# One queue for the turned pieces, pairs of groups four steps apart, and three smaller moves in a two-layer decoder trunk

## The chip, the core and the metric

The kernel runs on one core of one Trainium2 chip. The metric is the device time of one execution in microseconds, as the median of several runs. A profile comes from one execution of its own, taken with the hardware profiler.

The core's engines each run their instructions in order: TensorE (PE) multiplies matrices, VectorE (DVE) and ScalarE (ACT) work elementwise, GpSimd (POOL) and SyncE (SP) here only issue transfers. Transfers are also issued from ScalarE's queue. Each of these three has one queue of its own, and all of them move data over the same 16 DMA engines.

## The reference

Two layers over x of 256 tokens by 2048 features, all in float32:

```
layer 0:  h = rms_norm(x);  x += concat(mixer A(h), mixer B(h)) @ w_out     # gated spatial mixing, HGRN2 recurrence
          h = rms_norm(x);  x += (silu(conv3(h @ w_up)_a) * conv3(h @ w_up)_b) @ w_down
layer 1:  h = rms_norm(x);  x += (attention(h) * sigmoid(gate)) @ w_out     # 16 heads, QK-norm, forgetting bias
          h = rms_norm(x);  x += the same gated FFN with its own weights
```

Mixer A normalises its values v per head by their root mean square (a sum of squares over 128 columns) and mixes them along the tokens. In the attention, a logit per head and token gives log f; its cumulative sum c over the tokens enters the scores as c[t] - c[s]. The FFN has a hidden width of 5632, and conv3 is a causal convolution of width three along the tokens.

## The kernel before, in words

**Steps.** Every product of activations and weights is made from streamed weights. A weight tile w of 128x1024 (512 KB) is loaded on SP's queue (`weights`, L182, the load at L195), rounded by ScalarE into wh (L206), and VectorE makes the rest wl = w - wh (L211). The activations stand as such pairs too, and TensorE makes three products for each pair (L287 to L289 in `project_four`, L267 to L269 in `project_tok`), twelve matmuls of 512 columns for a tile. Such a tile is called a step here. In the mixers w has four buffers, and wh and wl three each; in the FFN every second tile uses a further pool with two of each (L182 to L190). The stationary operand is the activation, so the result has tokens in its partitions. A group of four output tiles (512 features) takes 8 steps over k = 0 to 15, and stands in two PSUM banks, one for each half of the tokens.

**Turning.** Where the next operation needs features in the partitions, the group is turned (`transposed`, L305): VectorE transposes blocks of 32x32 into a tile tmp (L308), and sixteen small transfers of 32 KB move the blocks across the partitions (L314). They go alternately to SP's queue and to GpSimd's, eight each. The last turned tile of the whole program uses three queues instead. In both FFNs tmp has one buffer, so the next tile can be transposed only when all sixteen pieces of the one before have landed. The turned tile is called turn in the mixers and zt in the FFN.

**Order.** A list of generators interleaves the work: `tick` (L121) runs once for each step and moves every pending generator on by one yield. After a tile is turned, its readers are put LAG = 6 steps later (LAST = 7 for the last group of a stage): the convolution in the FFN (L155 by way of `copy_in`, then L989 and L990), the scaled copies of queries and keys (also L155), the gates of the recurrence (L101), and the residual sum (L158) with the next norm's splits (L322, L326, L333, L336). A scheduler in the framework orders each engine's instructions within what the program's order and hand-written order edges leave free.

**Pairs.** The first two groups of an output projection and of an FFN's up-projection are interleaved (`project_pair`, L292), because they start before the last four k tiles of the activations are there: k 0 to 11 of the first (six steps), k 0 to 11 of the second, then k 12 to 15 of the first (two steps) and of the second. The first group so ends two steps before the second. The attention mixer starts in the same manner (L774): k 0 to 11 of the first queries, then of the first keys together with the gate columns (`keys_gate`, L754; its 528 columns take narrower matmuls, L770 and L771), then k 12 to 15 of both. In `keys_gate` the sixteen gate columns come on GpSimd's queue (L761), the rest on SP's (L762).

**Gate rows.** `forget` (L787) makes the cumulative sums, writes them to DRAM (L806) and loads them back into all 128 partitions, all sixteen heads in one transfer of 2 MB (L807). `attend` subtracts them from the scores.

**Values.** In mixer A the sums of squares of the values, their root and the scaling (L486 to L495) stand in the program directly, ahead of `mixes` (L510), which waits three ticks and then mixes a head per tick (L498).

**Start and end.** ScalarE's queue issues the first x tile, the norm's columns pp and the second x tile (L84 to L86), while SP's queue starts with the first weights. At the end, `add_y` (L1024) turns the FFN's last four groups, adds them to x (L158) and `finish_x` (L1048) sends x out; four of the output tiles are instead made feature by feature (L214, L1074 to L1077), so that they need no turning.

Of the kernel before, what the change touches and what calls it, by code (L numbers as in the profile page):

```python
# [8 lines left out]
F32 = mybir.dt.float32  # L9
# [3 lines left out]
ALU = mybir.AluOpType  # L13
AX = mybir.AxisListType

P = 128
S = 256
D = 2048
KT = D // P
NH = 8  # L20
# [6 lines left out]
LAST = 7  # L27
WAIT = 2
JOIN = 12
EPS = 1e-6  # L30
WARM = 7
AHEAD = {2: 2, 4: 4, 6: 6}
# [21 lines left out]
def tile_trunk(ctx: ExitStack, tc: tile.TileContext, x, pp_d, cst_d, mlev_d, msk_d,  # L54
               w_v, w_f, w_g, w_i, w_q, w_u, w_abo, w_cf, w_cqkv, w_cg, w_co, w_up, w_dn, spw_d, spb_d, out):
    nc = tc.nc
    V, SC, PE = nc.vector, nc.scalar, nc.tensor
# [10 lines left out]
    def nm(base):  # L68
        count[0] += 1
        return f"{base}_{count[0]}"  # L70
# [10 lines left out]
    ones = cp.tile([P, P], F32, tag="ones", name="ones")  # L81
    one1 = cp.tile([P, LANE], F32, tag="one1", name="one1")[:, 0:1]

    SC.dma_start(*fetch[0])  # L84
    SC.dma_start(pp[:, 0:C_FFN], pp_d[:, 0:C_FFN])
    SC.dma_start(*fetch[1])  # L86
    V.memset(ones, 1.0)
# [54 lines left out]
    def after(n, g):  # L142
        soon.append([n, g])
# [27 lines left out]
        while flight or queue or free or soon:  # L171
            tick()

    deep = {"pool": None, "turn": 0}

    def in_order(r, key="dma"):
        if key in deep:
# [113 lines left out]

    def project_pair(wa, wb, acts, shift=0):  # L292
        pa, pb = banks_for(), banks_for()
        for part in ((0, JOIN), (JOIN, KT)):
            for w4, ps in ((wa, pa), (wb, pb)):
                project_four(w4, acts, KT, shift=shift, ps=ps, part=part)
                if part[1] == KT:
                    yield ps

    def output(w, acts, shift=0):  # L300
        yield from project_pair(w[0:4], w[4:8], acts, shift)
# [3 lines left out]
    def transposed(src, tmp, dst, queues=None):  # L305

        for T in range(2):
            V.transpose(tmp.rearrange("p (b m i t) -> p b m i t", b=4, m=4, t=2)[:, :, :, :, T],  # L308
                        src(T).rearrange("p (m b j) -> p b m j", m=4, b=4))
        n = 2 * BLK  # L310
        for a in range(4):
            for b in range(4):
                qs = queues or (nc.sync, nc.gpsimd)
                qs[(a + b) % len(qs)].dma_start(dst[BLK * b:BLK * (b + 1), :, a * n:(a + 1) * n],  # L314
                                  tmp[BLK * a:BLK * (a + 1), b * 4 * n:(b + 1) * 4 * n]
                                  .rearrange("p (m r) -> p m r", m=4))
# [103 lines left out]
    def mixer_ab(norm):  # L420
# [61 lines left out]
                        .to_broadcast([P, NH, P]), ALU.mult)  # L482

        ss = hp.tile([P, LANE], F32, tag="ss", name="ss")
        for g in range(2):
            for T in range(2):  # L486
                i = (2 * g + T) * 4
                j = hp.tile([P, 512], F32, tag="smk", name=nm("junk"), bufs=1)
                sumsq(ss[:, i:i + 4], gv[g][:, T], j)
        rsq(ss[:, 0:2 * NH], ss[:, 0:2 * NH], P)  # L490
        for g in range(2):
            for T in range(2):
                i = (2 * g + T) * 4
                v4 = gv[g][:, T].rearrange("p (h d) -> p h d", d=P)
                V.tensor_tensor(v4, v4, ss[:, i:i + 4].unsqueeze(2).to_broadcast([P, 4, P]), ALU.mult)  # L495
        mg = [keep("mg") for _ in range(NH)]

        def mix(h):  # L498
# [9 lines left out]
                                   ALU.mult, ALU.add)  # L508

        def mixes():  # L510
            yield
            yield
            yield
            for h in range(NH):
                mix(h)
                yield
# [230 lines left out]
    def mixer_c(norm):  # L747
# [23 lines left out]
                        deep["main"] = PE.matmul(pb[T][:, 0:S], a_, t[:, CH + S:n], start=begin, stop=end)  # L771

        first = banks_for()
        for part in ((0, JOIN), (JOIN, KT)):  # L774
            project_tok(w_cqkv[0], norm, ps=first, part=part)
            keys_gate(part)
        drain()
        depth[0] = 2
        Rt = norm.Rt
# [3 lines left out]

        ct = hp.tile([P, 2, 2 * CH], F32, tag="ct", name="ct")[..., 0:CH]
        cb = hp.tile([P, CH * S], F32, tag="big", name="cb").rearrange("p (h s) -> p h s", s=S)

        def forget():  # L787
            f, fa, fc, on = (hp.tile([P, S], F32, tag=t, name=t)[0:CH] for t in ("f", "fa", "fc", "on"))
            ft = hp.tile([P, 2, LANE], F32, tag="ft", name="ft")
            V.memset(on, 1.0)  # L790
            for T in range(2):
                SC.activation(ft[:, T, 0:CH], pa[T][:, 0:CH], AF.Copy, scale=Rt[:, T:T + 1])
            yield
            ps = bank()
# [12 lines left out]
            nc.gpsimd.dma_start(cb, cd.partition_broadcast(P))  # L807
            yield
            ps = bank()
            for T in range(2):  # L810
                turn_in(ps[:, T * CH:(T + 1) * CH], fc[:, T * P:(T + 1) * P], ident[0:CH, 0:CH])
            V.tensor_copy(ct, ps[:, 0:2 * CH].rearrange("p (t c) -> p t c", t=2))
# [382 lines left out]
```

## Time and profile before

| | |
|---|---|
| time, median of 3 runs | 2315.13 us (2314.61 to 2317.67) |
| the profiled execution's own time | 2317.44 us |
| its span | 2315.7 us |
| TensorE busy (modelled ends) | 2292.7 us, 99% |
| VectorE, ScalarE, GpSimd busy | 67%, 57%, 15% |
| granted TensorE clock, mean | 0.996 |
| moved by DMA | 481 MB, 208 GB/s |
| pieces of turned tiles (L314) | 638 on SP, 637 on GpSimd, 5 on ScalarE |

The span is the part of the execution that the trace covers. In a timeline row stand the start in us from the span's start, the time in us, the engine, the line, the operation, output and input, the count of merged instructions, and in brackets how long the engine was idle before, with what ended it. SPq and ACTq are the queues' own issues. PEld is the weight load of TensorE, which overlaps the matmuls. Matmul times overlap too, since they are pipelined: the distance between two starts is what one costs.

### The profile page before, as it was taken

How to read it: one execution, taken by the hardware profiler on the slowest of the kernel's cores; microseconds unless marked ns; L12 is line 12 of the kernel's file. 1: busy time of each engine (PE TensorE's matmuls, PEld its weight loads, DVE VectorE, ACT ScalarE, POOL GpSimd, SP SyncE). 2: the span in 40 equal slices, each digit the busy share in tenths (PEclk: the TensorE clock that was granted, in tenths of full speed). 3: DMA queues.
4: the chain of work that ended last, by engine and by line, in shares of the span. 5: the costliest groups of instructions: out<-in, count | busy, mean ns of one | idle time of the engine just before them, and what ended most of it. 6: DMA issues, size and time to landing. Idle time of an engine off the chain costs nothing.

```text
span 2315.7 us, 31427 instructions
## 1 busy us (share of the span) xinstructions
PE 2292.7 (99%) x10370; PEld 1903.9 (82%) x10370; DVE 1557.9 (67%) x2369; ACT 1313.3 (57%) x1953; POOL 356.5 (15%) x661
## 2 busy tenths in 40 slices
PE   9999999999999999999989999999999999999999
PEld 7888887888888888888868888878888888888887
DVE  7788766777566657766756665657777467657666
ACT  7577655665455545654545556646655456456642
POOL 0101121122012002111211101121221022012102
PEclk9999999999999999999999999999999999999999
DMA  8755667777667657776666555767777677667765
GB/s 273 205 186 169 187 204 222 228 235 214 203 204 218 214 185 227 221 215 189 181 198 201 185 187 174 227 207 229 235 219 219 193 213 218 204 203 219 220 204 172
DMA packets 499204, 481.06 MB, mean 208 GB/s; under 512 B 116992, under 2 KB 468368, under 8 KB 498912
## 3 DMA queue, kind: packets, MB, share of 16 engines
q1 hardware_dynamic: 475344, 451.83, 62.5%
q0 software_dynamic: 21248, 23.69, 4.6%
q10 hardware_dynamic: 2448, 3.53, 0.5%
q8 instruction: 81, 1.33, 0.2%
q14 instruction: 83, 0.68, 0.1%
HBM read 434.85 MB, written 2.12 MB: 189 GB/s over the span
## 4 chain that ended last, share of the span: by engine, by line
PE 75%; DMA 2%; DVE 1%; SPq 1%; issue 0%; ACT 0%; DVEq 0%; ACTq 0%; POOLq 0%
PE pm L288 21%; PE pm L289 21%; PE pm L287 21%; PE pm L267 3%; PE pm L268 3%; PE pm L269 3%; SPq L314 1%; DMA zt<-tmp 1%; PE px L161 1%; PE px L770 1%; DMA turn<-tmp 0%; PE pm L771 0%; DVE wl L211 0%; DVE tmp L308 0%; PE px L164 0%
## 5 line engine op out<-in xcount | busy, mean ns | idle before, releaser
L211 DVE TENSOR_TENSOR wl<-w,wh 128x1024 fp32r<-128x1024 f32 (+1 forms) x812 | 986.7, 1218 | 655.6 <-ACT wh L206 650.0
L206 ACT ACTIVATE wh<-w 128x1024 fp32r<-128x1024 f32 (+1 forms) x812 | 854.6, 1054 | 796.3 <-PE pm L289 555.6
L288 PE MATMUL pm<-wl,a 128*128 128x512 f32 x1792 | 698.4, 390 | 2.9 <-DVE wl L211 2.9
L287 PE MATMUL pm<-wh,a 128*128 128x512 f32 x1792 | 701.0, 391 | 0.0
L289 PE MATMUL pm<-wh,a 128*128 128x512 f32 x1792 | 698.1, 390 | 0.0
L314 POOL DMA_DIRECT2D zt<-tmp x413 | 223.7, 549 | 1203.0 <-DVE tmp L308 1000.6
L288 PEld LDWEIGHTS pm<-wl,a 128*128 128x128 f32 x1792 | 336.8, 188 | 73.3 <-DVE wl L211 4.6
L289 PEld LDWEIGHTS pm<-wh,a 128*128 128x128 f32 x1792 | 336.6, 188 | 69.8
L287 PEld LDWEIGHTS pm<-wh,a 128*128 128x128 f32 x1792 | 336.7, 188 | 69.2
L288 PE MATMUL pm<-wl,hid 128*128 128x512 f32 x688 | 267.9, 389 | 0.0
L287 PE MATMUL pm<-wh,hid 128*128 128x512 f32 x688 | 267.9, 389 | 0.0
L289 PE MATMUL pm<-wh,hid 128*128 128x512 f32 x688 | 267.9, 389 | 0.0
L314 POOL DMA_DIRECT2D turn<-tmp x224 | 121.4, 550 | 635.3 <-DVE tmp L308 299.1
L267 PE MATMUL pm<-wh,a 128*128 128x512 f32 x464 | 184.3, 398 | 8.3 <-ACT wh L206 8.3
L268 PE MATMUL pm<-wl,a 128*128 128x512 f32 x464 | 181.9, 392 | 0.2 <-DVE wl L211 0.2
L269 PE MATMUL pm<-wh,a 128*128 128x512 f32 x464 | 181.6, 391 | 0.0
L289 PEld LDWEIGHTS pm<-wh,hid 128*128 128x128 f32 x688 | 129.2, 188 | 26.8
L287 PEld LDWEIGHTS pm<-wh,hid 128*128 128x128 f32 x688 | 129.2, 188 | 26.7
L288 PEld LDWEIGHTS pm<-wl,hid 128*128 128x128 f32 x688 | 129.2, 188 | 26.7
L155 ACT ACTIVATE conv<-zt,pp 128x256 f32<-128x256 f32 x176 | 95.6, 590 | 24.2 <-DMA zt<-tmp 23.0
L267 PEld LDWEIGHTS pm<-wh,a 128*128 128x128 f32 x464 | 87.6, 189 | 26.0 <-ACT wh L206 8.7
L308 DVE STREAM_TRANSPOSE tmp<-z 128x512 f32<-128x512 f32 x132 | 92.2, 706 | 18.4 <-ACT z L974 16.0
(217 smaller groups left out, 1935.3 us busy)
## 6 DMA issues: line engine op xcount, KB each, us to landing
w<-in_w_up SPq DMA_DIRECT2D x352, 512.0 KB, 4.5
w<-in_w_dn SPq DMA_DIRECT2D x176, 512.0 KB, 4.3
w<-in_w_cqkv SPq DMA_DIRECT2D x88, 512.0 KB, 4.3
w<-in_w_abo SPq DMA_DIRECT2D x32, 512.0 KB, 4.4
w<-in_w_cg SPq DMA_DIRECT2D x32, 512.0 KB, 4.0
w<-in_w_co SPq DMA_DIRECT2D x32, 512.0 KB, 4.0
zt<-tmp SPq DMA_DIRECT2D x414, 32.0 KB, 2.4
zt<-tmp POOLq DMA_DIRECT2D x413, 32.0 KB, 2.3
```

Of the source, the lines that this page charges most:

```text
L155: return behind(SC.activation(*args, **kw), "act")
L161: return behind(PE.matmul(*args, **kw), "main")
L206: deep["act"] = SC.activation(wh[:, p], w[:, p], AF.Copy)
L211: deep["sub"] = V.tensor_tensor(wl[:, p], w[:, p], wh[:, p].bitcast(F32), ALU.subtract)
L267: PE.matmul(ps[T], ah, h, start=k + i == 0, stop=False)
L268: PE.matmul(ps[T], ah, l, start=False, stop=False)
L269: deep["main"] = PE.matmul(ps[T], al, h, start=False, stop=k + i == KT - 1)
L287: PE.matmul(ps[T], ah, h, start=k + i == 0, stop=False)
L288: PE.matmul(ps[T], ah, l, start=False, stop=False)
L289: deep["mm"] = deep["main"] = PE.matmul(ps[T], al, h, start=False, stop=k + i == n - 1)
L308: V.transpose(tmp.rearrange("p (b m i t) -> p b m i t", b=4, m=4, t=2)[:, :, :, :, T], src(T).rearrange("p (m b j) -> p b m j", m=4, b=4))
L314: qs[(a + b) % len(qs)].dma_start(dst[BLK * b:BLK * (b + 1), :, a * n:(a + 1) * n], tmp[BLK * a:BLK * (a + 1), b * 4 * n:(b + 1) * 4 * n] ...
```

## The change

Five things change.

- `transposed`: all sixteen pieces of a turned tile are issued on GpSimd's queue. The last turned tile keeps its three queues.
- `project_pair` and the attention mixer's start: the second group stops at k tile 8 (HALF) before the first one ends. The order is: k 0 to 11 of the first, 0 to 7 of the second, 12 to 15 of the first, 8 to 15 of the second. The first group ends after 12 steps, the second after 16.
- `forget`: the gate rows come in four transfers of four heads each, the first at the next tick and each further one four ticks later, on GpSimd's queue as before.
- Mixer A's value sums become a generator, with a yield after each sum of squares and after the scaling of each group; `mixes` runs it in place of its three empty ticks.
- The first x tile is issued by SP's queue, and an order edge keeps the first weights behind it.

```diff
-    SC.dma_start(*fetch[0])
+    first_dma = nc.sync.dma_start(*fetch[0])
     SC.dma_start(pp[:, 0:C_FFN], pp_d[:, 0:C_FFN])
...
-    deep = {"pool": None, "turn": 0}
+    deep = {"pool": None, "turn": 0, "dma": first_dma}
...
-        for part in ((0, JOIN), (JOIN, KT)):
-            for w4, ps in ((wa, pa), (wb, pb)):
-                project_four(w4, acts, KT, shift=shift, ps=ps, part=part)
-                if part[1] == KT:
-                    yield ps
+        for w4, ps, part in ((wa, pa, (0, JOIN)), (wb, pb, (0, HALF)), (wa, pa, (JOIN, KT)), (wb, pb, (HALF, KT))):
+            project_four(w4, acts, KT, shift=shift, ps=ps, part=part)
+            if part[1] == KT:
+                yield ps
...
-                qs = queues or (nc.sync, nc.gpsimd)
+                qs = queues or (nc.gpsimd,)
...
+        def values():
+            for g in range(2):
+                for T in range(2):
...
+                    sumsq(ss[:, i:i + 4], gv[g][:, T], j)
+                    yield
+            rsq(ss[:, 0:2 * NH], ss[:, 0:2 * NH], P)
+            for g in range(2):
...
+                yield
...
         def mixes():
-            yield
-            yield
-            yield
+            yield from values()
...
-        for part in ((0, JOIN), (JOIN, KT)):
+        for part, other in (((0, JOIN), (0, HALF)), ((JOIN, KT), (HALF, KT))):
             project_tok(w_cqkv[0], norm, ps=first, part=part)
-            keys_gate(part)
+            keys_gate(other)
...
+        def rows(to, of):
+            nc.gpsimd.dma_start(to, of)
+            yield
...
-            nc.gpsimd.dma_start(cb, cd.partition_broadcast(P))
+            for g in range(4):
+                c = slice(4 * g, 4 * g + 4)
+                after(4 * g, rows(cb[:, c], cd[c].partition_broadcast(P)))
```

More of the change, by code (lines that the diff above doesn't have):

```diff
@@ L29 @@
 JOIN = 12
+HALF = 8
 EPS = 1e-6
@@ L484, in mixer_ab @@
         ss = hp.tile([P, LANE], F32, tag="ss", name="ss")
[L485 to L495, printed above, removed]
+        def values():
+            for g in range(2):
+                for T in range(2):
+                    i = (2 * g + T) * 4
+                    j = hp.tile([P, 512], F32, tag="smk", name=nm("junk"), bufs=1)
+                    sumsq(ss[:, i:i + 4], gv[g][:, T], j)
+                    yield
+            rsq(ss[:, 0:2 * NH], ss[:, 0:2 * NH], P)
+            for g in range(2):
+                for T in range(2):
+                    i = (2 * g + T) * 4
+                    v4 = gv[g][:, T].rearrange("p (h d) -> p h d", d=P)
+                    V.tensor_tensor(v4, v4, ss[:, i:i + 4].unsqueeze(2).to_broadcast([P, 4, P]), ALU.mult)
+                yield
         mg = [keep("mg") for _ in range(NH)]
```

## The prediction, made before the result was known

> **What bounds the kernel now.** I read the busy times first, then what TensorE waited for, then its timeline around each wait, then the SP and GpSimd queues there, and the end of VectorE's timeline.
>
> ```profile
> PE 2292.7 (99%) x10370; PEld 1903.9 (82%) x10370; DVE 1557.9 (67%) x2369; ACT 1313.3 (57%) x1953; POOL 356.5 (15%) x661
> ```
> ```profile
> PE pm L267 <- ACT wh L206: 8.3, 1, 8.3
> PE pm L288 <- DVE wl L211: 4.0, 6, 1.0
> PE pm L287 <- ACT wh L206: 3.3, 2, 2.0
> ```
> TensorE is busy 99% of the span, so nothing that another engine saves counts by itself. What can go is TensorE's own waits (microseconds, times, longest): nine in these rows, and three are large. Here they stand in TensorE's timeline, each with the row at which the normal pace is back:
>
> ```profile
> 355.10 0.73 PE L287 MATMUL pm<-wh,yb 128*128 128x512 f32 x2 [1.99 <-ACT wh L206]
> 360.34 0.40 PE L287 MATMUL pm<-wh,yb 128*128 128x512 f32 x1
> ...
> 1189.83 1.22 PE L267 MATMUL pm<-wh,a 128*128 128x512 f32 x2 [8.27 <-ACT wh L206]
> 1196.64 0.40 PE L267 MATMUL pm<-wh,a 128*128 128x512 f32 x1
> ...
> 1556.73 0.73 PE L287 MATMUL pm<-wh,yc 128*128 128x512 f32 x2 [1.35 <-ACT wh L206]
> 1562.21 0.40 PE L288 MATMUL pm<-wl,yc 128*128 128x512 f32 x1
> ```
> ```profile
> 1192.00:1194.00 2.00, 2.00 (x8) 1.73 (x8) 1.10 (x2) 1.06 (x1) 0.00 (x0) 0.50 0.89 285
> ```
> The last view's column before the DMA share is the granted clock: 0.50 just after the long wait. So a wait costs more than its idle time. Next, ScalarE at the pace of undisturbed work, and SP's queue:
>
> ```profile
> 1252.13 1.06 ACT L206 ACTIVATE wh<-w 128x1024 fp32r<-128x1024 f32 x1 [1.66 <-PE pm L269]
> 1254.85 1.06 ACT L206 ACTIVATE wh<-w 128x1024 fp32r<-128x1024 f32 x1 [1.66 <-PE pm L269]
> 1255.82 0.93 ACT L155 ACTIVATE qk<-turn,gq 128x256 f32<-128x256 f32 x2
> ```
> ```profile
> 338.19 11.80 SPq L314 DMA_DIRECT2D turn<-tmp  x16
> 503.00 5.11 SPq L314 DMA_DIRECT2D zt<-tmp  x8
> 1168.65 16.12 SPq L314 DMA_DIRECT2D turn<-tmp  x16
> 1540.46 11.16 SPq L314 DMA_DIRECT2D turn<-tmp  x16
> ```
> A step (one 512 KB weight tile, twelve wide matmuls) takes 1254.85 - 1252.13 = 2.72 us, so 0.227 us a matmul. With that the three waits cost:
> - **A**, at 355: 1.99 idle, then 5.24 us for 12 matmuls that normally take 2.72: 4.5 us.
> - **B**, at 1556: 1.35 idle, then 5.48 us for 13 matmuls (2.95 normally): 3.9 us.
> - **C**, at 1189: 8.27 idle, then 6.81 us at half clock, half of it lost: 11.7 us.
>
> Each stands shortly behind the only places where SP issues sixteen pieces in a row, two turned tiles back to back. SP also loads the weights, in order; for 11 to 16 us (four to six steps) no weight tile is asked for, and the casts L206 run dry. At C a second thing adds: the gate rows' broadcast holds the DMA engines ahead of the pieces.
>
> ```profile
> cb<-cd POOLq DMA_DIRECT2D x1, 2048.0 KB, 10.9
> ```
> That the clock falls after a short wait can be set against the Trainium skill, page "TensorE: Matmul & The Clock Gate", section "What's actually happening": half rate after an idle window of about 3.4 us. By that, A and B would lose only their idle time, 2.0 and 1.4 us, and the forecast would lie some 5 us higher; this trace shows 5.24 us for 12 matmuls after A, so the measurement decides.
>
> **The change part by part.** *Pieces on GpSimd alone.* All sixteen pieces of a turned tile now pass one queue.
>
> ```profile
> 503.27 4.33 POOL L314 DMA_DIRECT2D zt<-tmp  x8 [15.88 <-DVE tmp L308]
> 2284.60 3.25 POOL L314 DMA_DIRECT2D zt<-tmp  x6 [2.44 <-issue]
> ```
> ```profile
> zt<-tmp POOLq DMA_DIRECT2D x413, 32.0 KB, 2.3
> ```
> An issue costs 4.33 / 8 = 0.54 us, sixteen 8.66 us, where SP needed 5.11 for its half: the last piece goes out 3.6 us later. What goes is every piece on SP, so A, B and C lose their cause: -4.5 - 3.9 - 11.7 = -20.1. What is late next there is the weights' DMA itself, which keeps pace elsewhere.
>
> The cover for 3.6 us later pieces is how far the casts run ahead. In the FFN:
>
> ```profile
> L211 DVE TENSOR_TENSOR wl<-w,wh 128x1024 fp32r<-128x1024 f32 (+1 forms) x812 | 986.7, 1218 | 655.6 <-ACT wh L206 650.0
> ```
> ```profile
> 2289.29 1.06 ACT L206 ACTIVATE wh<-w 128x1024 fp32r<-128x1024 f32 x1 [1.66 <-PE pm L289]
> ...
> 2299.97 0.62 PE L232 MATMUL pm<-hid,wh 128*128 128x512 f32 x2
> ```
> A cast is made 10.7 us before TensorE uses it (the fourth-last weight tile). Take off the cast (1.06) and the subtraction behind it (1.22): 8 us of slack, so a conv that blocks ScalarE for 3.6 us costs nothing; without cover, up to 3.6 us for each FFN tile. In the mixers there are only three cast buffers: a cast starts when the step three before has ended, 2 x 2.72 = 5.4 us ahead, with 3.2 us of slack. There:
>
> ```profile
> 1248.03 1.30 DVE L308 STREAM_TRANSPOSE tmp<-z 128x512 f32<-128x512 f32 x2
> ```
> Pieces issued from 1249.6 on one queue have their last issue at 1249.6 + 15 x 0.54 = 1257.7 and land at 1260.0. If the copies L155 keep their place at 1255.82, ScalarE blocks for 4.2 us; its 1.8 us of copies end at 1261.9, cast and subtraction at 1264.2, and TensorE wants them at 1254.85 + 2.72 + 5.44 + 0.2 = 1263.2: 1.0 us lost. Bounds for the 28 mixer tiles: 0 (the program's order moves the readers behind the landing) to 28. Readers stand close to their landing in this trace, so the order seems made with the landing in view; nearest to that: **+2.5**.
>
> *Four steps apart.* The first tile of a pair ends after 12 steps instead of 14, the second still after 16; 4 x 2.72 = 10.9 us apart, just more than 8.66. The price: k tiles 12 to 15 are wanted after 10 steps, not 12, 5.4 us earlier. At the attention mixer's start:
>
> ```profile
> 1112.42 4.33 POOL L314 DMA_DIRECT2D zt<-tmp  x8 [6.08 <-DVE tmp L308]
> 1116.75 1.10 POOL L761 DMA_DIRECT2D w<-in_w_cf  x2
> ...
> 1126.59 0.28 PE L770 MATMUL px<-wh,a 128*128 128x272 f32 x1
> ...
> 1132.03 0.47 DVE L336 SCALAR_TENSOR_TENSOR a<-x,pp,a 128x256 fp32r<-128x256 f32 x1
> ```
> The last split (L336) ends at 1132.5; eight narrow steps of about 1.4 us behind 1126.59 put the new need at 1137.8. Covered by 5 us; gone, it would cost the excess. But the narrow gate weights (L761) stand on GpSimd's queue behind the last turned tile. That tile's sixteen pieces end at 1121 at best, and at 1124.4 when the single tmp buffer holds the chain of four tiles up: each then takes 1.3 (turning) + 0.3 (to the first issue) + 8.1 + 2.3 = 12.0 us against four steps, 10.9, and 3.3 us pile up. The first gate weight then lands at 1126.7 and its cast ends near 1127.4, against 1126.59: 0.8 us, then the subtraction behind it and some half clock. Bounds 0 (it goes ahead of the pieces) to 5, taken **+2**, near the row's sum.
>
> *Gate rows in four parts*: 2 MB once becomes four of 0.5 MB, 2.7 us each by 10.9 / 4, four steps apart, behind or between the pieces. GpSimd issues three more instructions (1.6 us). But the first q and k tiles still come together: 32 pieces, 17.3 us, on one queue. Bounds 0 to 9 (rival below); taken **+1**.
>
> *Values' sums in steps.* VectorE's burst of sums around 50 us delays one subtraction:
>
> ```profile
> 52.51 0.50 PE L288 MATMUL pm<-wl,a 128*128 128x512 f32 x1 [0.91 <-DVE wl L211]
> ```
> **-0.9**, bounds 0 and -1.2 (a second small wait there); the same operations run between later weights, and the mix matmuls come three steps later, long before their use. *First x tile*: it goes to SP's queue ahead of the first weights, so the norm columns go out one issue earlier:
>
> ```profile
> 1.18 0.45 ACTq L85 DMA_DIRECT2D pp<-in_pp  x1
> ...
> 5.23 0.35 DVE L335 TENSOR_SCALAR a<-x,pp 128x256 fp32r<-128x256 f32 x1 [4.22 <-DMA pp<-in_pp]
> ```
> L335, on which the first real matmul waits, starts 0.45 us earlier; the first weights go one issue (0.45) later: **-0.4**, bounds -0.5 and +0.5.
>
> *The end* has no cover: tmp is one buffer, and the last four tiles chain through it.
>
> ```profile
> 2268.24 1.30 DVE L308 STREAM_TRANSPOSE tmp<-y 128x512 f32<-128x512 f32 x2
> 2279.20 1.30 DVE L308 STREAM_TRANSPOSE tmp<-y 128x512 f32<-128x512 f32 x2
> 2288.80 1.28 DVE L1089 TENSOR_TENSOR y<-y,pm 128x512 f32<-128x512 f32 x2
> 2292.24 1.31 DVE L308 STREAM_TRANSPOSE tmp<-y 128x512 f32<-128x512 f32 x2 [2.16 <-DMA zt<-tmp]
> 2301.50 1.31 DVE L308 STREAM_TRANSPOSE tmp<-y 128x512 f32<-128x512 f32 x2 [0.54 <-DMA out<-x]
> 2309.16 1.43 DVE L158 TENSOR_TENSOR x<-x,zt 128x256 f32<-128x256 f32 x4 [0.68 <-DMA zt<-tmp]
> 2311.03 0.78 DVE L1077 TENSOR_TENSOR x<-x,pm 128x256 f32<-128x256 f32 x2
> ```
> At 12.0 us a tile: 2268.2, 2280.3, 2292.3, 2304.4. The last, on three queues as before, has its sums 7.66 us later (2309.16 - 2301.50), at 2312.1, and the last L1077 ends near 2314.7 against 2311.8: +2.9. A GpSimd pause like the 2.44 us above, in this chain, adds 2.4 (it comes about every 106 issues; three tiles hold 48). Bounds 2.9 and 7.5; taken **+4**.
>
> Sum: -20.1 - 0.9 - 0.4 + 2.5 + 2 + 1 + 4 = **-11.9**. The profiled execution took 2317.4 us (2315.7 span and 1.7 around it): 2305.5. The median of the runs, 2315.1, lies 2.3 lower: forecast **2303**.
>
> **Rivals.** (1) *Nothing is given back* except the end's 2.9: -18.5, **2296.6**. For it: the FFN's 8 us of slack. Against: the gate weights behind sixteen pieces.
> (2) *C returns in another form.* The 32 pieces end at 1168.7 + 17.3 = 1186.0 and land near 1188.3; TensorE ran dry at 1181.6. If the copies of the first keys stand ahead of the cast that TensorE needs, up to 7 us and half clock behind it come back, 9 to 10: **2312.5**.
> (3) *Slower: the readers in the mixers keep their places.* 28 tiles at 1.0 us each instead of 2.5 in all: +25.5, **2328**. It decides from (21.4 - 7) / 28 = 0.5 us a tile. For it: 3.2 us of slack is less than 4.2. Against: the order seems to follow the landings, and not every reader comes so early.
> (4) *The change doesn't do what it says: GpSimd can't issue at 0.54 us while VectorE works.* Doubled, a tile takes 17 us and even the FFN's slack is gone: 4 us for some 50 tiles, far above **2400**. Eight issues took 4.33 us with VectorE 67% busy, so 2%. The Trainium skill, "SBUF — State Buffer", section "SBUF: two separate sides", speaks for it: GpSimd cannot write descriptors while VectorE is in a two-port mode. Here the row of 4.33 us shows no such hold.
>
> **How the numbers follow.** Forecast 0.54 (2298 to 2308), rival 1 0.12, rival 2 0.18, rival 3 0.14, rival 4 0.02. A measurement here tells about 0.2%, 4.6 us. Faster by more: 0.54 + 0.12 and the part of rival 2 in which less than all returns, 0.06: **0.72**. Within: the rest of rival 2, **0.12**. Slower: **0.16**. Low end 2294: no pause in the end and no new wait. High end 2318: rival 2 with the end at its upper bound. Left out: rivals 3 and 4 and a little below.
>
> **What would show it.** Right: no wait near A, B and C, no L314 on SP; GpSimd's groups as x16 in 8.7 us; last L308 rows 12 us apart; the out transfer 3 us or more behind TensorE's last matmul compared with now. Wrong: new waits of TensorE on wh at L267 in the mixers behind L155 or L101 that wait for turn, a wait at the first L770, or GpSimd's spacing above 0.54.

## The result, and the profile after

The changed kernel takes **2326.45 us** (median of 5 runs, 2324.97 to 2330.79), the kernel before, on the same chip, 2314.61 us (5 runs, 2310.87 to 2317.67). The ratio is 1.0057, with a 95% interval of 1.004 to 1.0073: slower by 0.6%. The forecast was 2303, with a range that ends at 2318. The profiled execution was the longest of the five, 2330.79 us; its span is 2328.7, 13.0 above that of the execution profiled before.

The page's row of busy times, then TensorE's waits by what it waited for (total, times, longest), then the pieces' landing times, all of the changed kernel:

```profile
PE 2292.9 (98%) x10370; PEld 1898.6 (82%) x10370; DVE 1554.3 (67%) x2369; ACT 1302.7 (56%) x1953; POOL 703.5 (30%) x1296
```
```profile
PE pm L289 <- DVE wl L212: 6.6, 8, 1.3
PE px L773 <- ACT wh L766: 3.7, 2, 3.0
PE pm L269 <- DVE wl L212: 3.4, 5, 0.8
```
```profile
zt<-tmp POOLq DMA_DIRECT2D x821, 32.0 KB, 4.2
turn<-tmp POOLq DMA_DIRECT2D x448, 32.0 KB, 4.3
```

The wait of 8.3 us on `wh` is gone, and the 2.0 and 1.4 us too; in their place stand many small ones. TensorE's busy time has not moved, and its share has fallen from 99 to 98%: 13 us are idle that were not. A piece now lands 4.2 us after its issue, where it was 2.3.

To find the 13 us, the span is cut where TensorE's timeline has a border that both kernels show: the first matmul, the first on `ya`, the last on `yb`, the first and the last with 272 columns (the attention mixer's first step with gate columns), the first and the last on `yc`, the next first one on `hid`, the end of TensorE's last matmul, the end of the span. The forecast column sorts the prediction's terms into these stages (the mixers' readers, +2.5, put with C).

| stage, us | before | after | difference | forecast |
|---|---|---|---|---|
| to the first matmul | 5.73 | 5.45 | -0.3 | -0.4 |
| first mixer, to its output product | 292.81 | 295.53 | +2.7 | -0.9 |
| its output product (A) | 91.88 | 86.81 | -5.1 | -4.5 |
| first FFN | 736.17 | 734.49 | -1.7 | 0 |
| attention mixer's first step | 29.28 | 39.97 | **+10.7** | +2 |
| on to the output product (C) | 344.94 | 336.44 | -8.5 | -8.2 |
| its output product (B) | 91.24 | 88.21 | -3.0 | -3.9 |
| second FFN up to the first `hid` | 174.80 | 180.67 | **+5.9** | 0 |
| to TensorE's last matmul | 544.50 | 544.73 | +0.2 | 0 |
| after TensorE's last matmul | 4.35 | 16.40 | **+12.1** | +4 |
| span | 2315.7 | 2328.7 | +13.0 | -11.9 |

One border does not cut the same work in both kernels. In the changed kernel TensorE takes 24 of the wide matmuls for the first queries (L268 to L270) behind the first narrow one (L773), which stood ahead of it before; at 0.227 us each they move 5.4 us from the first FFN's stage into the next. The first narrow one and its neighbours, of the changed kernel:

```profile
1118.92 0.39 PE L270 MATMUL pm<-wh,a 128*128 128x512 f32 x1
1122.28 0.39 PE L773 MATMUL px<-wh,a 128*128 128x272 f32 x1 [2.97 <-ACT wh L766]
...
1123.20 0.58 PE L268 MATMUL pm<-wh,a 128*128 128x512 f32 x1 [0.16 <-ACT a L333]
```

So these two stages have to be read together: 765.5 us before, 774.5 after, +9.0 where +2 was forecast. The other stages hold the same matmuls in both kernels.

A, B and C gave what was forecast. Three places took back far more: the end (+12.1 for +4), the attention mixer's start (+9.0 for +2) and the second FFN's start (+5.9 for 0), and the first mixer a little. At the end of the changed kernel, first VectorE's rows, then GpSimd's issues, then TensorE's last matmul:

```profile
2269.20 1.30 DVE L308 STREAM_TRANSPOSE tmp<-y 128x512 f32<-128x512 f32 x2
...
2284.36 1.30 DVE L308 STREAM_TRANSPOSE tmp<-y 128x512 f32<-128x512 f32 x2
...
2300.64 0.68 DVE L1098 TENSOR_TENSOR y<-y,pm 128x512 f32<-128x512 f32 x1
2301.24 1.30 DVE L308 STREAM_TRANSPOSE tmp<-y 128x512 f32<-128x512 f32 x2
...
2315.35 1.31 DVE L308 STREAM_TRANSPOSE tmp<-y 128x512 f32<-128x512 f32 x2 [4.50 <-DMA zt<-tmp]
...
2323.13 1.43 DVE L159 TENSOR_TENSOR x<-x,zt 128x256 f32<-128x256 f32 x4 [5.16 <-DMA out<-x]
```
```profile
2271.07 7.61 POOL L314 DMA_DIRECT2D zt<-tmp  x14 [56.01 <-issue]
2279.02 1.09 POOL L314 DMA_DIRECT2D zt<-tmp  x2 [0.35 <-DMA zt<-tmp]
2286.24 8.68 POOL L314 DMA_DIRECT2D zt<-tmp  x16 [6.12 <-ACT wh L207]
2302.83 1.63 POOL L314 DMA_DIRECT2D zt<-tmp  x3 [7.91 <-DVE tmp L308]
2306.82 7.04 POOL L314 DMA_DIRECT2D zt<-tmp  x13 [2.36 <-issue]
2316.94 2.71 POOL L314 DMA_DIRECT2D zt<-tmp  x5 [3.08 <-DVE tmp L308]
```
```profile
2312.02 0.28 PE L229 MATMUL pm<-hid,wl 128*128 128x256 f32 x1
```

The transposes stand 15.2, 16.9 and 14.1 us apart, and TensorE ends a group every 10.9. Three things make up the distances. In the first, the sixteen issues take 9.0 us (GpSimd stops once for 0.35 until an earlier piece has landed), and the next transpose starts 4.2 us behind the last (2284.36 - 2280.11), right behind a subtraction on VectorE; the pieces took 4.0 us to land. In the third, GpSimd pauses for 2.36 us, and the trace names nothing that it waited for. The second is odd: its pieces are out at 2294.9, yet the next transpose starts only at 2301.24, and no DMA is named. It stands in VectorE's order behind L1098, which waits for TensorE's last group to be turned. That is taken up below.

### The profile page after: what moved, and what is told of

The parts are those of the page before. It is cut to its first block, busy times and chain, and to the rows that moved or that the text cites. A ratio compares the mean times of both kernels' runs of the same rounds, so it can differ in the third digit from the quotient of the medians.

```text
span 2328.7 us, 30630 instructions
## 1 busy us (share of the span) xinstructions
PE 2292.9 (98%) x10370; PEld 1898.6 (82%) x10370; DVE 1554.3 (67%) x2369; ACT 1302.7 (56%) x1953; POOL 703.5 (30%) x1296
## 5 line engine op out<-in xcount | busy, mean ns | idle before, releaser
L314 POOL DMA_DIRECT2D zt<-tmp x821 | 446.4, 552 | 999.1 <-DVE tmp L308 778.1
L289 PEld LDWEIGHTS pm<-wl,a 128*128 128x128 f32 x1792 | 336.9, 188 | 78.3 <-DVE wl L212 9.4
L314 POOL DMA_DIRECT2D turn<-tmp x448 | 243.9, 552 | 510.4 <-DVE tmp L308 161.1
L288 PEld LDWEIGHTS pm<-wh,a 128*128 128x128 f32 x1792 | 336.9, 188 | 70.3 <-ACT wh L207 0.9
L290 PEld LDWEIGHTS pm<-wh,a 128*128 128x128 f32 x1792 | 336.6, 188 | 70.1
L268 PE MATMUL pm<-wh,a 128*128 128x512 f32 x464 | 183.7, 397 | 0.3 <-ACT wh L207 0.2
L270 PE MATMUL pm<-wh,a 128*128 128x512 f32 x464 | 182.1, 393 | 0.0
L269 PEld LDWEIGHTS pm<-wl,a 128*128 128x128 f32 x464 | 87.5, 189 | 24.3 <-DVE wl L212 7.0
L998 DVE SCALAR_TENSOR_TENSOR conv<-zt,pp,conv 128x255 f32<-128x255 f32 x176 | 80.9, 479 | 34.4 <-ACT conv L156 34.2
```

The costliest lines, as they stand in the source:

```text
L268: PE.matmul(ps[T], ah, h, start=k + i == 0, stop=False)
L269: PE.matmul(ps[T], ah, l, start=False, stop=False)
L270: deep["main"] = PE.matmul(ps[T], al, h, start=False, stop=k + i == KT - 1)
L288: PE.matmul(ps[T], ah, h, start=k + i == 0, stop=False)
L289: PE.matmul(ps[T], ah, l, start=False, stop=False)
L290: deep["mm"] = deep["main"] = PE.matmul(ps[T], al, h, start=False, stop=k + i == n - 1)
```

## The experiments

Theory 1: the one queue is the loss, since a turned tile then holds the single buffer tmp longer than TensorE takes for a group, and the tiles at the end of an FFN pile up. Rival: another part is the loss, above all the pairs' new ends. All kernels were timed in five rounds beside the kernel before; each result is the median and the ratio to that kernel with its 95% interval. Distances between kernels of different rounds are taken from the ratios, by 2315 us. The stages of their profiled executions (the first FFN and the first step are to be added up; in after, e2, e3, e5 and e13 the 24 matmuls have moved from the one to the other):

| us | first mixer | A | first FFN | first step | C | B | second FFN | end |
|---|---|---|---|---|---|---|---|---|
| before | 292.8 | 91.9 | 736.2 | 29.3 | 344.9 | 91.2 | 174.8 | 4.4 |
| after | 295.5 | 86.8 | 734.5 | 40.0 | 336.4 | 88.2 | 180.7 | 16.4 |
| e1_two_queues | 298.3 | 87.5 | 735.7 | 29.4 | 343.8 | 87.9 | 174.8 | 3.9 |
| e2_only_pieces | 293.3 | 88.5 | 736.5 | 38.3 | 335.6 | 89.7 | 175.8 | 16.4 |
| e3_tail_two | 296.6 | 86.8 | 734.0 | 39.2 | 337.4 | 87.7 | 178.5 | 3.5 |
| e4_tmp2 | 294.3 | 88.3 | 736.0 | 30.0 | 336.6 | 88.4 | 178.6 | 5.4 |
| e5_cf_sp | 296.5 | 87.1 | 733.1 | 40.0 | 341.0 | 87.5 | 179.5 | 15.9 |
| e6_only_pairs | 293.7 | 86.8 | 735.2 | 29.4 | 343.9 | 86.8 | 174.8 | 5.0 |
| e7_ffn_two | 292.8 | 87.0 | 736.2 | 29.7 | 334.8 | 87.9 | 175.4 | 3.3 |
| e8_ffn_two_values | 292.1 | 86.8 | 735.3 | 29.7 | 335.6 | 87.9 | 177.7 | 3.3 |
| e9_qk_only | 293.0 | 87.3 | 735.1 | 29.4 | 334.1 | 86.8 | 175.1 | 3.7 |
| e10_rows_in_one | 294.3 | 87.2 | 735.2 | 29.4 | 334.1 | 86.8 | 174.8 | 3.8 |
| e11_values_in_steps | 293.4 | 86.9 | 735.1 | 29.4 | 334.4 | 86.8 | 175.2 | 3.9 |
| e12_before_tail_one | 293.4 | 91.8 | 736.0 | 29.3 | 344.3 | 90.8 | 174.8 | 14.2 |
| e13_turn_first | 292.1 | 86.8 | 734.0 | 39.5 | 337.1 | 88.0 | 179.0 | 11.4 |
| e14_tail_one_turn_first | 293.2 | 91.6 | 736.0 | 29.3 | 343.9 | 89.4 | 174.8 | 11.4 |
| e15_only_values | 292.6 | 91.8 | 736.0 | 29.3 | 344.5 | 91.2 | 174.8 | 4.5 |

### The queue undone, and the queue alone

**e1_two_queues**: the changed kernel, pieces alternating again.

```diff
-                qs = queues or (nc.gpsimd,)
+                qs = queues or (nc.sync, nc.gpsimd)
```


> The changed kernel with one part undone: pieces alternate between SP and GpSimd again; groups four steps apart, gate rows in four, values in steps and first x stay. Theory 1 (one queue is the loss: sixteen pieces in series, 4.2 us to land instead of 2.3, behind a single buffer): the end after TensorE's last matmul falls from 16.4 us back to 4 to 5 us, the attention mixer's first step loses its 9 us, and A and B come back (about 8 us of waits), C at least in part: 2311 to 2318 us. Rival (the other parts, above all the interleaved groups, are the loss): 2322 us or more, with the long end gone or not.

2309.01 us, 0.9964 (0.9951 to 0.9978): faster than before, and 22 us below the whole change. End and first step are back, but A and B did not return, which theory 1 had expected. C did, in another form. In TensorE's and SP's timelines and the window behind the first wait, of this kernel:

```profile
1186.61 2.93 PE L162 MATMUL px<-qk 128*128 128x128 f32 x8 [4.16 <-ACT qk L156]
1192.69 0.50 PE L269 MATMUL pm<-wl,a 128*128 128x512 f32 x1 [2.18 <-DVE wl L212]
```
```profile
1169.55 11.88 SPq L314 DMA_DIRECT2D turn<-tmp  x16
```

```profile
1186.00:1190.00 4.00, 3.31 (x9) 2.41 (x10) 1.17 (x4) 2.25 (x4) 0.00 (x0) 0.57 1.00 375
```

The sixteen pieces still block SP for 11.9 us; a wait of 4.2 us on `qk`, one of 2.2 us and a clock of 0.57 (the column ahead of the DMA share) follow.

**e2_only_pieces**: the kernel before, with that line changed the other way and nothing else.

> The kernel before with one part done alone: all pieces on GpSimd's queue. Theory 1: the end is 14 to 17 us after TensorE's last matmul, A and B are gone, the attention mixer starts late: 2322 to 2330 us, as the whole change. Rival (other parts are the loss): 2303 to 2314 us, with the three waits gone and little given back.

2323.77 us, 1.0026 (1.0014 to 1.0039). Theory 1 holds: the queue alone makes the end 16.4 us, costs 9.3 us at the attention mixer's start (both stages together) and takes C away, though the gate rows come in one broadcast here. Of A and B it takes 3.3 and 1.5 us.

**e6_only_pairs**: the kernel before, with the pairs' new ends alone (`project_pair` and the attention mixer's start as in the change).

> The kernel before with one part done alone: interleaved groups end four steps apart. Theory 3 (from the run with two queues everywhere, in which A and B were gone without one queue: it is the four steps between the ends, not the queue, that takes them away): A and B gone, C stays, end unchanged; 2307 to 2311 us. Rival (A and B went there by another part): 2313 us or more. If the first mixer's output product starts at 301 us or later in this run too, the pairs cause that loss and not the values' sums (rival of theory 2).

2306.99 us, 0.9964 (0.9952 to 0.9977). A and B are gone by the pairs alone, 5.1 and 4.4 us; C stays:

```profile
1185.51 1.22 PE L268 MATMUL pm<-wh,a 128*128 128x512 f32 x2 [7.60 <-ACT wh L207]
```

So the rival falls: the pairs are a gain. The four steps between two groups' ends also put four steps between two turned tiles, and SP gets weights out between them; for A and B no queue has to change. SP's queue at A, of this kernel:

```profile
334.25 5.10 SPq L314 DMA_DIRECT2D turn<-tmp  x8
339.46 1.63 SPq L196 DMA_DIRECT2D w<-in_w_abo  x3
345.13 5.10 SPq L314 DMA_DIRECT2D turn<-tmp  x8
```

By the ratios the queue alone costs 6 us and the pairs alone gain 8, yet the whole change costs 13. The two do not add up: both take from A and B, which can go only once, and the second FFN's start loses most where both meet.

### Where the queue costs: the end

**e12_before_tail_one**: the kernel before, with all sixteen pieces of the last FFN's turned tiles but the last on GpSimd's queue (24 of 1280 pieces change queue; the expectation's 1313 is a slip).

```diff
-                       (nc.sync, SC, nc.gpsimd) if end else None)
+                       (nc.sync, SC, nc.gpsimd) if end else (nc.gpsimd,) if last else None)
```


> The kernel before with one edit: the last feed-forward block's three turned tiles of the output sum send all sixteen pieces on GpSimd's queue; 24 of 1313 pieces change queue, nothing else. Theory 1 (the long end is made by these tiles alone): the end after TensorE's last matmul 13 to 17 us instead of 4.35, 2323 to 2329 us, as slow as the whole change. Rival (the end is long only together with the earlier tiles on the same queue or the other parts): end under 9 us, 2314 to 2319 us.

2325.26 us, 1.0043 (1.003 to 1.0056): 24 transfers on another queue cost 10 us. Its transposes stand 15.1, 16.9 and 12.5 us apart:

```profile
2267.49 1.30 DVE L308 STREAM_TRANSPOSE tmp<-y 128x512 f32<-128x512 f32 x2
...
2282.61 1.30 DVE L308 STREAM_TRANSPOSE tmp<-y 128x512 f32<-128x512 f32 x2
...
2299.53 1.30 DVE L308 STREAM_TRANSPOSE tmp<-y 128x512 f32<-128x512 f32 x2
...
2312.03 1.31 DVE L308 STREAM_TRANSPOSE tmp<-y 128x512 f32<-128x512 f32 x2 [2.90 <-DMA zt<-tmp]
```

**e3_tail_two**: the changed kernel with the converse edit, SP and GpSimd in turn for these tiles alone.

> The changed kernel, with the last feed-forward block's tiles of the output sum (three of them, before the last one, which has three queues anyway) on SP and GpSimd in turn as before; every other tile stays on GpSimd alone. Theory 1 (the chain through the one transpose buffer at the end costs 12 us, because each tile takes 14 to 17 us with pieces in series on one queue): the end after TensorE's last matmul falls from 16.4 to 4 to 6 us, transposes L308 stand 12 us or the pace of TensorE's groups apart, 2314 to 2317 us. Rival (the end is long because of the order in which VectorE's work was written out, or because the earlier end of TensorE only moved the wait): it stays over 12 us, 2323 us or more.

2318.17 us, 1.0006 (0.9996 to 1.0016), within 0.2% of before and 12 us below the whole change. The end is 3.5 us; its last two transposes, at 2289.05 and 2299.93 us, stand 10.9 us apart, TensorE's own pace:

```profile
2289.05 1.30 DVE L308 STREAM_TRANSPOSE tmp<-y 128x512 f32<-128x512 f32 x2
...
2299.93 1.31 DVE L308 STREAM_TRANSPOSE tmp<-y 128x512 f32<-128x512 f32 x2
```

**e4_tmp2**: the changed kernel with two buffers, everything still on GpSimd.

```diff
-            return (hp.tile([P, 1024], F32, tag="tmp", name=nm("tmp"), bufs=1),
+            return (hp.tile([P, 1024], F32, tag="tmp", name=nm("tmp"), bufs=2),
...
-            c = hp.tile([P, S], F32, tag="conv", name=nm("conv"), bufs=6)
+            c = hp.tile([P, S], F32, tag="conv", name=nm("conv"), bufs=5)
```


> The changed kernel with two buffers instead of one for the feed-forward blocks' transposes (room for it by five convolution buffers instead of six); pieces all on GpSimd still. Theory 1 (pieces in series hurt because the next transpose must wait for the last piece to leave the one buffer): the end after TensorE's last matmul falls from 16.4 to 6 to 10 us, and the attention mixer's first step (40 us, against 29.3 before) comes down by 5 us or more: 2310 to 2319 us. Rival (what hurts is the time that a tile's own pieces take on one queue, 8.7 us and 4.2 to land, or GpSimd's pace): end and first step gain under 3 us each, 2322 to 2330 us.

2307.25 us, 0.9962 (0.9949 to 0.9976), 22 us below the whole change, better than expected. One more buffer cures both the end (5.4 us) and the attention mixer's start (0.6 us above the kernel before, both stages together), with GpSimd's issues as slow as before. So it is not the queue's pace by itself but that pace in a chain through one buffer. In GpSimd's timeline at the first step the gate weights still stand behind sixteen pieces, and it does no harm there. Below are their rows and TensorE's first narrow matmul in e4, then the gate weights' row in the changed kernel:

```profile
1110.07 8.66 POOL L314 DMA_DIRECT2D zt<-tmp  x16 [2.93 <-DVE x L159]
1118.72 2.15 POOL L764 DMA_DIRECT2D w<-in_w_cf  x4
...
1123.98 0.28 PE L773 MATMUL px<-wh,a 128*128 128x272 f32 x1
```
```profile
1118.29 2.24 POOL L764 DMA_DIRECT2D w<-in_w_cf  x4
```

The first gate weights go out at the same time in both. What differs is TensorE's order: here it asks for them at 1124.0, in the changed kernel at 1119.3 (1122.28 - 2.97), ahead of the 24 wide matmuls.

**e13_turn_first** and **e14_tail_one_turn_first**: order edges on VectorE's late sums and subtractions in the changed kernel, and the same edges in e12's, so that the third transpose at the end no longer stands behind the sum that waits for TensorE.

```diff
+            if "late" in deep:
+                tc.add_manual_dep(deep["sub"].ins, deep["late"].ins.name, order, reason="behind the turn")
...
-                        V.tensor_tensor(d, d, ps[T], ALU.add)
+                        r = V.tensor_tensor(d, d, ps[T], ALU.add)
+                        if last and final and q:
+                            tc.add_manual_dep(r.ins, deep["turned"].ins.name, order, reason="behind the turn")
```


> The changed kernel with an order edge on VectorE at the end: the sums of the last group into y, and the last two weight tiles' subtractions, stand behind the transpose of the group before (in the changed kernel that transpose, at 2301.24 us, stands behind a sum that waits for TensorE until 2300.6, though its buffer was free near 2296.3: sixteen pieces from 2286.24 to 2294.9 and 1.9 us to land at that place). Theory 5 (of the 12 us at the end, some 5 are VectorE's written order and the rest the pace of one queue): that transpose starts 4 to 5 us earlier, the end after TensorE's last matmul falls from 16.4 to 11 to 12.5 us, 2320 to 2323 us. Rival (the pieces' pace alone): end over 15 us, 2325 us or more.

> The same order edge in the kernel before with its last three turned tiles on one queue (there 2325.26 us, the transpose at 2299.53 us behind a sum, the buffer free near 2295). Theory 5: end 9 to 10.5 us instead of 14.2, 2319 to 2322 us. Rival: 13 us or more, 2324 us or more.

2319.92 us, 1.0028 (1.0015 to 1.004), and 2321.69 us, 1.0024 (1.0014 to 1.0035). The end falls to 11.4 us in both. The transposes of e13 (the inserted lines shift L308 to L310):

```profile
2278.41 1.30 DVE L310 STREAM_TRANSPOSE tmp<-y 128x512 f32<-128x512 f32 x2
...
2290.38 1.31 DVE L310 STREAM_TRANSPOSE tmp<-y 128x512 f32<-128x512 f32 x2 [1.01 <-DMA zt<-tmp]
...
2304.91 1.30 DVE L310 STREAM_TRANSPOSE tmp<-y 128x512 f32<-128x512 f32 x2
```

The distance of 16.9 us has become 12.0 (2290.38 - 2278.41), and now a DMA ends the wait. So of the 12 us at the end, 5 were VectorE's order, which the framework's scheduler wrote anew when the pieces went to one queue, and 7 came with the pace of the pieces, GpSimd's pause of 2.36 us among them, which e13 has too. In e14 the edges took less, 2.8 of e12's 9.8 us, and its end missed the 9 to 10.5 expected.

### Where the queue costs: the attention mixer's first step

**e5_cf_sp**: the changed kernel with the gate weights on SP's queue.

```diff
-                nc.gpsimd.dma_start(w[:, 0:CH], w_cf[:, k * P:k * P + CH])
+                nc.sync.dma_start(w[:, 0:CH], w_cf[:, k * P:k * P + CH])
```


> The changed kernel, with the gate weights of the attention mixer's first step (w_cf, 16 loads of 8 KB) on SP's queue, out of the way of the pieces on GpSimd's. Theory 1a (these loads stand behind sixteen pieces of the last turned query tile, and that is the 9 us that the attention mixer's start lost): the wait of 3 us on wh and the half clock behind it go, the first step ends 5 to 9 us earlier, 2317 to 2321 us. Rival (the step is late because of the order of the groups or of the turned tiles themselves): the step gains under 2 us, 2325 to 2328 us.

2331.9 us, 1.0054 (1.0041 to 1.0068). The expectation failed: the wait of 3 us on `wh` is gone, yet the first FFN and the step together take 773.1 us, 1.4 less than in the changed kernel and 7.7 more than in the kernel before. TensorE, in this kernel, now comes to the last k tiles and waits there for a cast and for the activations:

```profile
1143.28 0.40 PE L773 MATMUL px<-wh,a 128*128 128x272 f32 x1 [1.25 <-ACT wh L766]
1144.88 0.50 PE L268 MATMUL pm<-wh,a 128*128 128x512 f32 x1 [0.84 <-ACT a L333]
```

The first FFN's last turned tile feeds these, at the end of the same chain through one buffer. Its transposes in e5 and in the kernel e7, which follows (two queues in both FFNs):

```profile
1077.38 1.30 DVE L308 STREAM_TRANSPOSE tmp<-y 128x512 f32<-128x512 f32 x2
1092.57 1.31 DVE L308 STREAM_TRANSPOSE tmp<-y 128x512 f32<-128x512 f32 x2
1109.91 1.30 DVE L308 STREAM_TRANSPOSE tmp<-y 128x512 f32<-128x512 f32 x2
1125.33 1.30 DVE L308 STREAM_TRANSPOSE tmp<-y 128x512 f32<-128x512 f32 x2
```
```profile
1073.34 1.30 DVE L308 STREAM_TRANSPOSE tmp<-y 128x512 f32<-128x512 f32 x2
1084.66 1.31 DVE L308 STREAM_TRANSPOSE tmp<-y 128x512 f32<-128x512 f32 x2 [0.36 <-DVE y L1098]
1095.58 1.30 DVE L308 STREAM_TRANSPOSE tmp<-y 128x512 f32<-128x512 f32 x2
1104.90 0.71 DVE L308 STREAM_TRANSPOSE tmp<-y 128x512 f32<-128x512 f32 x1 [0.30 <-DVE y L1098]
```

From the first to the last it is 48.0 us in e5 and 31.6 in e7. The late gate weights were what TensorE met first; they are worth the 1.4 us, and the chain the rest. (C's stage is 4.6 us longer in e5 than in the changed kernel; that was not followed up.)

### Putting the queue where it pays

**e7_ffn_two**: the changed kernel, with two queues for both FFNs' tiles (the two calls of `transposed` there get `(nc.sync, nc.gpsimd)`). **e8_ffn_two_values**: also the values' sums in one go again.

> The changed kernel with all the feed-forward blocks' pieces on SP and GpSimd in turn as before, the mixers' pieces on GpSimd alone. Theory 1 (one queue costs where a feed-forward block's tiles chain through one buffer, and gains only in the mixers, at C above all): end back to 4 to 5 us, attention mixer's first step back to 29 to 30 us, second block's start back to 175 us, and the gain at C (8 us) kept, so below the run with two queues everywhere (2309.0 us): 2299 to 2306 us. Rival (the late first step and the gain at C are two sides of one thing, the order of the groups there): C's wait comes back or the first step stays late, 2308 to 2315 us.

> As the run with two queues in the feed-forward blocks alone, and the values' sums again in one go, as in the kernel before. Theory 2 (the first mixer lost 2 to 5 us, first output product at 301 to 304 us instead of 298.5, because the values' sums stand between casts of its groups): 2 to 5 us faster than that run, the waits on wl and wh at 54 and 75 us go. Rival (these waits come from the pairs' new ends, four steps apart): same within 1 us or slower by 1 us, the waits stay.

2302.67 us, 0.9948 (0.9936 to 0.9961), and 2298.81 us, 0.9934 (0.9921 to 0.9947). The end and the first step are mended, the second FFN's start in part (175.4 and 177.7 us, though the two kernels differ only in mixer A's values, far ahead of it), and C's gain stays. (Both have a wait of 2 us on `wl` behind a late weight tile near 2208 us; it was not followed up.)

**e9_qk_only**: GpSimd alone only for the attention mixer's turned queries and keys; all else on two queues, pairs, gate rows and first x as changed, values as before.

```diff
-                qs = queues or (nc.gpsimd,)
+                qs = queues or (nc.sync, nc.gpsimd)
...
-            transposed(lambda T: z[:, T], flat(piece("tmp", 2)), heads(t))
+            transposed(lambda T: z[:, T], flat(piece("tmp", 2)), heads(t), (nc.gpsimd,))
```


> GpSimd's queue alone only where C was: the pieces of the attention mixer's turned query and key tiles, behind the gate rows. All other pieces on SP and GpSimd in turn; groups four steps apart, gate rows in four parts, first x first; values' sums in one go as before. Theory 1 (C is the one place that needs the one queue; A and B go by the groups' ends, and output tiles of the mixers on one queue cost the second feed-forward block's start up to 3 us): A, B, C gone, second block's start at 174.8 us, end at 4 to 5 us: 2295 to 2300 us, as fast as the run with one queue in all mixers (2298.8) or 1 to 3 us faster. Rival (one queue was needed at other mixer tiles too): a wait at A or B or a new one, 2302 us or more.

**2296.63 us, 0.9917 (0.9903 to 0.993)**: with e10, which equals it, the fastest of all, 19 us below the kernel before in the same rounds and 32 below the change. SP's queue at C, of this kernel, has weights only, and TensorE's waits there are gone:

```profile
1150.54 46.98 SPq L196 DMA_DIRECT2D w<-in_w_cqkv  x18
```

**e10_rows_in_one**: e9 with the gate rows in one broadcast. **e11_values_in_steps**: e9 with the values in steps. **e15_only_values**: the kernel before with the values in steps alone.

> As the run with one queue for query and key tiles only, and the gate rows' broadcast in one DMA of 2 MB again. Theory 4 (C goes because the pieces leave SP's queue, and the four parts are worth nothing by themselves: with pieces alone on GpSimd and one broadcast the stage took 335.6 us, with four parts 336.4): within 1.5 us of that run. Rival (the four parts let the pieces through): the stage behind the first step takes 338 us or more instead of 335, and the run is 3 to 9 us slower.

> As the run with one queue for query and key tiles only, and the values' sums in steps, as in the changed kernel. Theory 2 (steps cost: first output product of the first mixer 292 to 294 us after the first matmul without, 293 to 298 with them): 2 to 4 us slower, with waits on wl and wh between 50 and 80 us. Rival (these differences come from how fast the first weights land in a given execution, and not from the values): within 1 us in the median.

> The kernel before with one part done alone: the values' sums in steps. Theory 2 (steps cost the first mixer something): from the first matmul to the first output product 294 us or more instead of 292.8, the median 1 to 4 us above the kernel before. Rival (execution to execution differences in how the first weights land): within 1 us of the kernel before, or the forecast's 0.9 us below it.

2296.26 us, 0.9918 (0.9905 to 0.9932); 2300.05 us, 0.9928 (0.9915 to 0.9942); 2316.08 us, 1.0002 (0.9993 to 1.0011). The gate rows in four parts are worth nothing: 334.1 us at C with and without. The values neither gain nor cost in the kernel before, and in e11 the profiled stages are those of e9 within 0.5 us. The medians of e7 and e11 do lie 3 to 4 us above those of e8 and e9, as theory 2 (e8's expectation) had it, but the intervals overlap, and no stage shows it. The first mixer's stage lies between 292.1 and 298.3 us over all these executions; e13, whose first mixer is that of the changed kernel (295.5), has 292.1. What moves it stays open.

## Why the prediction was wrong, point by point

- **A, B and C**: right in size (-5.1, -3.0, -8.5 with what came back, against -4.5, -3.9 and -8.2), wrong in the part of the change that brings two of them. The prediction let every piece's leaving SP take all three and gave the pairs only a price; e6 shows that the pairs' ends alone take A and B (5.1 and 4.4), where the queue alone takes 3.3 and 1.5 (e2). So for A and B the forecast was right by luck: another part of the change brought them. One reading was also loose: the 5.24 us behind A hold a second wait of 0.52 us on `wl`. C needs the queue (e1, e6 against e2, e9), and there the whole stage moves by 9.7 us (343.9 in e6, 334.1 in e9), near the 11.7 of the forecast.
- **The end, taken at +4 with 7.5 as its upper bound: the mis-sized term, +12.1.** The mechanism was right, the single tmp and the chain of tiles. The 12.0 us a tile hold only where nothing else comes in (e13's second distance is 12.0, e12's last 12.5); here the distances were 15.2, 16.9 and 14.1, some 10 us more in all. About 3 of these are the first tile, whose pieces took 4.0 us to land: the prediction carried over 2.3 us from a row in which only eight pieces followed each other on a queue. About 5 are VectorE's order, which it kept as it was (e13), and 2 the pause, which it allowed for. Its upper bound of 7.5 stands there without a sum; 2.9 and one pause of 2.4 make 5.3.
- **"Eight microseconds of slack" for the FFN, cost 0**: failed at its two ends. The slack was that of the weight casts and says nothing of the tiles' own chain. The prediction worked that chain out for the attention mixer's start, but only to date the gate weights there (+2). What was lost there, 9.0 us over both stages, came with the chain itself: with two buffers 0.6 us of it are left (e4), with two queues 0.4 (e7), with the gate weights on SP's queue 7.7 (e5). The wait at the first narrow matmul, named as a sign of being wrong, did come, but not as reckoned: the first gate weights went out at 1118.3, ahead of the last tile's pieces and not at 1124.4 behind them, and TensorE's order asked for them 24 wide matmuls earlier.
- **Second FFN's start, 0 against +5.9**: the up-projection's first tiles. It is +0.0 with two queues everywhere, whether or not the pairs are changed (e1, e6), +1.0 with one queue alone (e2), 3.7 to 5.9 where both meet, two buffers or not (the changed kernel, e3, e4, e5, e13), and 0.6 and 2.9 with one queue in the mixers alone (e7, e8). In the changed kernel four waits on `wl` and `wh` stand in it, 3.1 us together; what makes the casts late there was not taken apart, so the cause of this term stays open.
- **Rival 3, readers in the mixers that keep their places**: not what happened. e7 and e8 have all the mixers' tiles on GpSimd's queue, e9 only the queries and keys; they take 0.6 and 1.4 us more than e9 at C and 1.1 more at B. So the mixers' other tiles cost some 2 us, near the +2.5, read from single executions.
- **Rival 2**: no part of it; 32 pieces on GpSimd's queue at C leave TensorE no wait in e9. **Rival 4**: an issue took 0.54 us again (8.68 / 16).
- **Gate rows +1, values -0.9, first x -0.4**: 0, 0 and -0.3.

Together the two chains missed by 8.1 and 7.0 us, the second FFN's start by 5.9 and the first mixer by 3.6, the other stages by 0.3 in sum: 24.9 us, from -11.9 to +13.0.

## What to carry to other kernels

A transfer that is moved to relieve one queue lengthens the other's turn; look for the places where a single buffer makes that turn a chain, above all at the ends of stages, where nothing hides it, and measure such a chain by the distance between two of its own links, not by slack that belongs to other work. Undo a bundle part by part: here one part brought A and B, one place of another brought C, and that part's other places lost all of it again. Where a scheduler orders the engines, a change of a queue also changes the order on engines that it does not touch, here VectorE's at the end and TensorE's at the attention mixer's start, and with it what a stage border cuts.

## What the runs showed of the hardware

- **Landing depends on what else moves.** At the end of the changed kernel a piece of 32 KB took 4.0 us from issue to landing in the first tile, among weight loads (2.1 MB beside them in the 11 us from 2270), and 1.9 in the second, with less beside them (1.0 MB in the 10 us from 2286); the median over the kernel is 4.2. The Trainium skill, page "DMA: Bandwidth & Descriptors", section "Anatomy of one DMA — SWDGE (gpsimd) path", fits one DMA with 2.0 us and a little for its bytes, which makes 2.1 us for 32 KB, an estimate. The second tile's 1.9 us agree, the median of 4.2 is twice that. In e7 the pieces that pass one queue (the mixers') take 4.4 us, those that go to two (the FFNs') 2.6, in the same execution; why one queue makes them so much later was not tried.
- **GpSimd pauses** of 2.0 to 2.5 us with no releaser named stand about 106 issues apart, or twice that: 4 show in the kernel before and 10 in the changed one, where GpSimd issues twice as many transfers (the last stands ahead of the row at 2306.82 above). Why was not tried.
- **The clock falls after short waits.** After the 2.97 us wait in the attention mixer's first step the granted clock, the column ahead of the DMA share, is 0.85 and 0.81 in the two windows of 5 us below, which adds to the loss there. In the kernel before it is 0.50 from 357 to 360 us, behind waits of 1.99 and 0.52 us. The two windows of the changed kernel:

```profile
1120.00:1125.00 5.00, 2.56 (x9) 1.93 (x10) 4.01 (x10) 2.87 (x7) 2.94 (x6) 0.85 0.31 76
1125.00:1130.00 5.00, 5.00 (x20) 4.05 (x19) 2.91 (x7) 1.46 (x3) 5.00 (x10) 0.81 0.44 112
```
